# A four-layer encoder in split float32: the output product of each FFN takes both parts of an input tile in one 512-column matmul

## The chip, the cores and the metric

One Trainium2 chip; the kernel runs on one of its NeuronCores. The metric is the device time in microseconds of one execution, and the times given are medians of several timed executions. The engines that matter here are TensorE (PE, with its weight loads as PEld), VectorE (DVE), ScalarE (ACT) and the queue of SyncE (SP) that issues the weight transfers.

## What is computed

Four layers over 256 tokens of width 1024, in float32. Each layer is a half-step SwiGLU FFN, a token mixer (attention, spatial gating, differential attention, attention again) and a second half-step FFN, each between two RMS norms:

```python
D_MODEL, SEQ, DEPTH, D_FF = 1024, 256, 4, 2816

def swiglu(h, w_in, w_out):
    gate, up = jnp.split(h @ w_in, 2, axis=-1)
    return (jax.nn.silu(gate) * up) @ w_out

def reference(x, norm_g, ...):
    for i in range(DEPTH):
        g = norm_g[i]
        x = x + 0.5 * rms_norm(swiglu(rms_norm(x, g[0]), ff1_w_in[i], ff1_w_out[i]), g[1])
        h = rms_norm(x, g[2])
        m = (mixer_a, mixer_b, mixer_c)[i % 3](h, ...)
        x = x + rms_norm(m, g[3])
        x = x + 0.5 * rms_norm(swiglu(rms_norm(x, g[4]), ff2_w_in[i], ff2_w_out[i]), g[5])
    return x
```

The change is in the last product of `swiglu`, which runs eight times (two FFNs in each of four layers).

## The kernel before

Activations lie transposed: 128 features on the partitions, the 256 tokens (`S`) in the free dimension, so a vector of 1024 features is 8 tiles (`KD`) and the hidden layer of 2816 features is 22 tiles (`NJ`). Every large product is made of three: each operand is split into a high part, rounded to the type float32r, and a low part, the rest in the same type, and PE adds high by high, high by low and low by high in PSUM. A matmul takes a 128x128 block of weights as its stationary operand and the 256 tokens of an input tile as its moving operand; each is preceded by its own weight load (LDWEIGHTS).

The weights come as a stream (class `Stream`): SP transfers 1 MB tiles `w_raw` (L104), ACT casts a piece of 1024 columns into `w_hi` (L127), DVE subtracts to get `w_lo` (L130). A piece holds 8 blocks of 128x128. There are 8 slots for split pieces (`SLOTS`); `W.done()` after a piece's last matmul lets ACT and DVE split the piece that goes into the slot made free.

An FFN (`ffn`) has two stages. The first (`project_pair`, L501 and L482) makes gate and up in pairs of tiles; `gate` takes their product and splits the hidden tiles into a high part `hh` (L528, ACT) and a low part `hl` (L529, DVE). They lie in four tiles of SBUF, `h0` and `h1` for the high parts and `l0` and `l1` for the low ones; the mixers use the same four tags for other data. The second stage, which I call the output product, loops over 8 output tiles `d`, and for each over 22 input tiles `k`. `mm3` issues three matmuls for each `k`: `w_hi` by `hh` (L166), `w_lo` by `hh` (L167), `w_hi` by `hl` (L168), 256 columns each. So a stage has 8 x 22 x 3 = 528 matmuls, and because a piece has 8 blocks and a tile 22, piece borders fall inside the tiles at changing places.

When a tile is summed, `Branch.tile_done` has ACT square it out of PSUM (L352) and scale it into `yg` (L353), and DVE adds the square to a running sum (L363). Where a later stage's input can be begun ahead (`Ahead`), ACT and DVE then split two tiles more (L386, L387). After the eighth tile a chain of small steps forms the norm, and the next stage begins with those prepared matmuls (L425 or L427). PSUM tiles of two banks come from a pool of three (`pair()`).

The order of the work on PE, DVE and ACT is the order in which the program is written (`manual_schedule`); each engine runs its own queue in that order and waits on semaphores. `mm3` also serves the last four tiles of the mixers' output product (`project_out`) and one product of `mixer_b`. The gMLP and attention stages have matmuls of other shapes, among them 512-column ones in class `Wide` (L622; an input tile is stationary there and a block of weights of 512 columns moves), and transposes (L694).

Of the kernel before, what the change touches and what calls it, by code (L numbers as in the profile page):

```python
# [16 lines left out]
P = 128  # L17
# [39 lines left out]
def encoder_trunk_kernel(  # L57
# [107 lines left out]
    def mm3(o, ah, al, bh, bl, start, stop, skip=False):  # L165
        nc.tensor.matmul(o, ah, bh, start=start, stop=False, skip_group_check=skip)  # L166
        nc.tensor.matmul(o, al, bh, start=False, stop=False, skip_group_check=skip)  # L167
        nc.tensor.matmul(o, ah, bl, start=False, stop=stop, skip_group_check=skip)  # L168
# [79 lines left out]
    class Normed:  # L248


        def __init__(self, update, gain):
            self.h = act.tile([P, KD, S], F32R, tag="xh", name="xh")
            self.l = act.tile([P, KD, S], F32R, tag="xl", name="xl")
# [86 lines left out]
    class Branch:  # L340


        def __init__(self, gain, n=None, ahead=None):

            self.gain, self.n, self.ahead = gain, n, ahead

        def tile_done(self, d, ps):
            if d == 0:
                self.yg = act.tile([P, KD, S], F32, tag="yg", name="yg")
                self.acc = tmp.tile([P, S], F32, tag="ysq", name="ysq", bufs=1)  # L350
            sq = tmp.tile([P, S], F32, tag="sq1", name="sq1") if d > 0 else self.acc
# [115 lines left out]

    def blocks(piece):
        return [part.rearrange("p (k c) -> p k c", k=KD) for part in piece]

    def project_pair(n, together, between=lambda piece: None, finish=lambda ps: None, most=2, warm=None):

        if together:
            ps = n.ahead.ps
            ws = [blocks(W.peek(i)) for i in range(4)]
            for k, low in JOIN:
                for i in range(4):
# [3 lines left out]
                    for part in ws[i][:1] if low else ws[i]:  # L481
                        nc.tensor.matmul(  # L482
                            o, part[:, k, :], (n.l if low else n.h)[:, k, :],
# [5 lines left out]
        else:  # L489
            ps = pair()  # L490
            for i in range(4):
                wh, wl = blocks(W.peek())
                o = ps[:, i // 2, i % 2 * S:(i % 2 + 1) * S]
                passes = ((wh, n.h), (wh, n.l), (wl, n.h))
# [4 lines left out]
                for at, (k, m) in enumerate(order):  # L499
                    part, xs = passes[m]  # L500
                    nc.tensor.matmul(o, part[:, k, :], xs[:, k, :], start=(at == 0), stop=(at == 3 * KD - 1))  # L501
                    if warm and i == 0:
                        warm(DUMMY[at])
# [7 lines left out]
    def ffn(l, which, update, ahead):  # L511
        n = Normed(update, g_sb[:, l, 4 * which, :])
        hs = [large(tag, (n, S), F32R) for tag, n in (("h0", 16), ("h1", 6), ("l0", 8), ("l1", 14))]

        def hidden(k, n=1):
            h, l = (hs[0], k) if k < 16 else (hs[1], k - 16), (hs[2], k) if k < 8 else (hs[3], k - 8)
            return [t[:, a:a + n, :] for t, a in (h, l)]
# [3 lines left out]
        def gate(jp, ps):  # L521
# [5 lines left out]
            hh, hl = hidden(2 * jp, 2)  # L527
# [24 lines left out]
        for d in range(KD):  # L552
            o = pair()[:, 0, 0:S]
            for k in range(NJ):
                wh, wl = blocks(W.peek())
                hh, hl = hidden(k)
                mm3(o, wh[:, b, :], wl[:, b, :], hh[:, 0, :], hl[:, 0, :], start=(k == 0), stop=(k == NJ - 1))
                b += 1
                if b == KD:
                    if d == KD - 1 and k == NJ - 1:  # L560
# [3 lines left out]
            br.tile_done(d, o)  # L564
# [4 lines left out]
    def project_out(parts, l, between, ahead):  # L569
# [4 lines left out]
        for k, low in ORDER:  # L574
            if not low:
                between(k)
            x = parts(k)[low]
            for (wh, wl), o in zip(ws, os):
                for part in (wh,) if low else (wh, wl):
                    nc.tensor.matmul(  # L580
                        o, part[:, k, :], x, start=(k == 0 and part is wh and not low), stop=(k == KD - 1 and low),
                        skip_group_check=True,
# [7 lines left out]
        for d in range(4, KD):  # L590
            o = pair()[:, 0, 0:S]
            wh, wl = blocks(W.peek())
            for k in range(KD):
                oh, ol = parts(k)
                mm3(o, wh[:, k, :], wl[:, k, :], oh, ol, start=(k == 0), stop=(k == KD - 1))
# [8 lines left out]
    def joined(early, outs):  # L604

        def parts(k, n=None):
            return [x[:, k % 4] if n is None else x[:, k % 4:k % 4 + n] for x in (early if k < 4 else outs)]
# [153 lines left out]
    def mixer_a(l, i, update):  # L761
# [65 lines left out]
        def mix(j):  # L827

            if j == 0:
                t = large("l0", (KD, S), F32R)  # L830
                early.extend((t[:, 0:4], t[:, 4:8]))
# [3 lines left out]
        def between(k):  # L835

            ahead.x_parts(k)
            if k == 0:
                outs.extend(
                    act.tile([P, 4, S], F32R, tag=tag, name=name) for tag, name in (("xh", "oh"), ("xl", "ol"))  # L840
                )
# [13 lines left out]
    def mixer_b(l, i, update):  # L855
# [42 lines left out]
        oh, ol = large("h0", (KD, S), F32R), large("h1", (KD, S), F32R)  # L898
# [29 lines left out]
        for jp in range(KD // 2):  # L928
            ps = pair()
            for e in range(2):  # L930
                wh, wl = blocks(W.peek())
                for k in range(KD):
# [267 lines left out]
```

## Time and profile before

| | |
|---|---|
| median of 3 timed executions | 1996.17 us (1995.66 to 1996.88) |
| the profiled execution's own time | 1993.93 us |
| its span, first to last instruction | 1992.1 us |
| PE busy | 1978.3 us, 16227 matmuls |
| DVE busy | 1279.4 us, 1689 instructions |
| ACT busy | 1081.5 us, 1610 instructions |
| mean granted TensorE clock | 0.998 |
| read from HBM | 347.44 MB, 175 GB/s over the span |

The profile is of one execution, and durations are compared with its own time, not with the median of the others. Matmuls are pipelined: the duration given for one (283 ns for 256 columns) is longer than the distance from its start to the start of the next. What a stream of matmuls costs is therefore read from the distance of starts, and the busy time of PE is the union of overlapping spans. A "granted clock" of 1.0 means 2.4 GHz.

### The profile page before, as it was taken

The page shows a single profiled execution, that of the slowest core. Times are in us where ns is not written, and L with a number is a line of the kernel's source. Part 1 is how long each engine was busy: PE and PEld are TensorE (multiplying, and loading weights), DVE is VectorE, ACT ScalarE, POOL GpSimd, SP SyncE. Part 2 cuts the span into 40 slices and gives each one's busy share as a digit, 9 for nine tenths or more (in the row PEclk, how much of TensorE's full clock was granted, in tenths as well). Part 3 has the DMA queues.
Part 4 walks back from the last instruction along what each step waited for, and adds up shares of the span by engine and source line. Part 5 has one row for each costly group of instructions (what it writes and reads, how often), then busy time and mean ns, then how long its engine had stood idle before and what let it go on. Part 6 is the DMA issues. An engine that isn't in the chain of part 4 may idle for free.

```text
span 1992.1 us, 37700 instructions
## 1 busy us (share of the span) xinstructions
PE 1978.3 (99%) x16227; PEld 1949.1 (98%) x16227; DVE 1279.4 (64%) x1689; ACT 1081.5 (54%) x1610; POOL 6.5 (0%) x21
## 2 busy tenths in 40 slices
PE   9999999999999999999999999999999999999998
PEld 9999999999999989999999999999999999999998
DVE  7655867655765577765665568775566655868553
ACT  6454656545544555645554555764555455666452
POOL 0000000000000000000000000000000000000000
PEclk9999999999999999999999999999999999999999
DMA  7545524645445553645455444254445454525541
GB/s 277 196 170 197 186 99 178 224 169 181 172 177 191 190 173 127 233 170 192 148 194 202 176 151 170 107 225 178 173 154 203 182 192 159 201 113 193 195 184 43
DMA packets 50502, 350.91 MB, mean 176 GB/s; under 512 B 5760, under 2 KB 6016, under 8 KB 9120
## 3 DMA queue, kind: packets, MB, share of 16 engines
q1 hardware_dynamic: 48096, 341.86, 46.7%
q10 hardware_dynamic: 2160, 6.52, 0.9%
q8 instruction: 127, 2.08, 0.4%
q14 instruction: 39, 0.32, 0.0%
q0 software_dynamic: 80, 0.13, 0.0%
HBM read 347.44 MB, written 1.05 MB: 175 GB/s over the span
## 4 chain that ended last, share of the span: by engine, by line
PE 97%; DVE 1%; DMA 1%; ACT 1%; issue 0%; ACTq 0%; SPq 0%; DVEq 0%
PE pp_t L501 54%; PE pp_t L166 9%; PE pp_t L168 9%; PE pp_t L167 9%; PE pp_t L482 3%; PE pp_t L622 3%; PE pp_t L580 2%; PE pp_t L662 1%; DMA w_raw<-in_w 1%; PE pp_t L427 1%; PE pst_t L694 1%; PE pst_t L427 1%; PE pst_t L225 1%; PE pst_t L240 1%; PE pp_t L425 0%; PE pp_t L816 0%
## 5 line engine op out<-in xcount | busy, mean ns | idle before, releaser
L127 ACT CAST w_hi<-w_raw 128x1024 fp32r<-128x1024 f32 (+1 forms) x649 | 670.4, 1047 | 504.5 <-PE pp_t L501 299.3
L130 DVE TENSOR_TENSOR w_lo<-w_raw,w_hi 128x1024 fp32r<-128x1024 f32 (+1 forms) x649 | 774.9, 1219 | 210.1 <-ACT w_hi L127 203.4
L501 PE MATMUL pp_t<-xh,w_hi 128*128 128x256 f32 x2976 | 527.7, 284 | 0.7 <-ACT w_hi L127 0.7
L501 PE MATMUL pp_t<-xl,w_hi 128*128 128x256 f32 x2976 | 524.4, 283 | 0.2 <-DVE xl L316 0.2
L501 PE MATMUL pp_t<-xh,w_lo 128*128 128x256 f32 x2976 | 523.9, 283 | 0.0
L501 PEld LDWEIGHTS pp_t<-xh,w_hi 128*128 128x128 f32 x2976 | 430.1, 192 | 2.6 <-ACT w_hi L127 1.4
L501 PEld LDWEIGHTS pp_t<-xl,w_hi 128*128 128x128 f32 x2976 | 430.7, 192 | 0.7 <-DVE xl L316 0.4
L501 PEld LDWEIGHTS pp_t<-xh,w_lo 128*128 128x128 f32 x2976 | 430.7, 192 | 0.1
L166 PE MATMUL pp_t<-h,w_hi 128*128 128x256 f32 x1456 | 412.0, 283 | 0.0
L167 PE MATMUL pp_t<-h,w_lo 128*128 128x256 f32 x1456 | 412.0, 283 | 0.0
L168 PE MATMUL pp_t<-l,w_hi 128*128 128x256 f32 x1440 | 407.5, 283 | 0.0
L166 PEld LDWEIGHTS pp_t<-h,w_hi 128*128 128x128 f32 x1456 | 279.6, 192 | 0.0
L167 PEld LDWEIGHTS pp_t<-h,w_lo 128*128 128x128 f32 x1456 | 279.6, 192 | 0.0
L168 PEld LDWEIGHTS pp_t<-l,w_hi 128*128 128x128 f32 x1440 | 276.5, 192 | 0.0
L523 DVE TENSOR_TENSOR gs<-pp_t,rbc 128x512 f32<-128x512 f32 x88 | 60.7, 690 | 97.3 <-PE pp_t L501 97.3
L363 DVE TENSOR_TENSOR ysq<-ysq,sq 128x256 f32<-128x256 f32 x72 | 30.6, 425 | 128.4 <-ACT sq L352 128.3
L526 DVE TENSOR_TENSOR hf<-pp_t,gs 128x512 f32<-128x512 f32 x88 | 60.9, 692 | 65.5 <-ACT gs L524 65.5
L529 DVE TENSOR_TENSOR l<-hf,h 128x512 fp32r<-128x512 f32 x88 | 61.0, 693 | 60.4 <-ACT h L528 60.4
L524 ACT ACTIVATE gs<-gs 128x512 f32<-128x512 f32 x88 | 55.6, 632 | 75.7 <-DVE gs L523 75.7
L528 ACT CAST h<-hf 128x512 fp32r<-128x512 f32 x88 | 54.5, 619 | 66.7 <-DVE hf L526 66.7
L301 ACT ACTIVATE xh<-xr,g_sb 128x256 fp32r<-128x256 f32 x96 | 44.8, 504 | 59.4 <-DVE xr L458 56.5
L679 ACT ACTIVATE ex<-s,nm 128x128 f32<-128x128 f32 x96 | 42.7, 448 | 43.1 <-DVE nm L671 24.9
(191 smaller groups left out, 1709.9 us busy)
## 6 DMA issues: line engine op xcount, KB each, us to landing
w_raw<-in_w SPq DMA_DIRECT2D x322, 1024.0 KB, 4.8
l<-in_a_bias ACTq DMA_DIRECT2D x8, 512.0 KB, 7.5
w_raw<-in_w SPq DMA_DIRECT2D x3, 512.0 KB, 7.5
out_y<-xr SPq DMA_DIRECT2D x4, 256.0 KB, 2.5
xr<-in_x_t SPq DMA_DIRECT2D x2, 384.0 KB, 5.8
w_raw<-in_w SPq DMA_DIRECT2D x2, 256.0 KB, 4.3
l<-in_b_ws ACTq DMA_DIRECT2D x1, 512.0 KB, 5.4
l<-in_b_ln_g ACTq DMA_DIRECT2D x1, 512.0 KB, 7.0
```

Source lines behind the costliest of these rows:

```text
L127: nc.scalar.copy(hi[:, cols], raw[:, cols])
L130: nc.vector.tensor_tensor(lo[:, cols], raw[:, cols], hi[:, cols].bitcast(F32), op=ALU.subtract)
L166: nc.tensor.matmul(o, ah, bh, start=start, stop=False, skip_group_check=skip)
L167: nc.tensor.matmul(o, al, bh, start=False, stop=False, skip_group_check=skip)
L168: nc.tensor.matmul(o, ah, bl, start=False, stop=stop, skip_group_check=skip)
L482: nc.tensor.matmul(o, part[:, k, :], (n.l if low else n.h)[:, k, :], start=((k, low) == JOIN[0] and i == 2 and part is ws[i][0]), stop=((k ...
L501: nc.tensor.matmul(o, part[:, k, :], xs[:, k, :], start=(at == 0), stop=(at == 3 * KD - 1))
L523: nc.vector.tensor_tensor(gs, ps[:, :, 0:S], n.bc.unsqueeze(1).broadcast_to([P, 2, S]), op=ALU.mult)
L524: nc.scalar.activation(gs, gs, AF.Silu)
L526: nc.vector.tensor_tensor(hf, ps[:, :, S:2 * S], gs, op=ALU.mult)
L529: nc.vector.tensor_tensor(hl, hf, hh.bitcast(F32), op=ALU.subtract)
L622: nc.tensor.matmul(self.ps[:, t, :], xs[:, kk, t * P:(t + 1) * P], ws, start=((kk, low) == self.order[0] and ws is wh and not (t == 0 and ...
```

## The change

In the output product of the FFN, for its first seven tiles `d`, one matmul with 512 moving columns takes the high and the low part of an input tile together against the same block of `w_hi`; the columns of the high part are summed in one half of a PSUM bank and those of the low part in the other half (`product2`). The matmuls with `w_lo` add to the first half. Within a piece of weights, all 512-column matmuls come first, then all those with `w_lo`. The two halves are added when the tile is done (`Branch.joined`): ACT copies the second half to SBUF, DVE adds it to the first into `yg`, and square and scale then read `yg` in place of PSUM. The eighth tile keeps three matmuls of 256 columns for each input tile (`product`, in the order high by high, high by low, low by high), and no halves to be added.

So that both parts can move in one instruction, they lie side by side: the normed input is one tile `xp` in place of `xh` and `xl`, and the hidden tiles lie as pairs in the four tags by ranges of `k` (0 to 7 in `h0`, 8 to 11 in `h1`, 12 to 15 in `l0`, 16 to 21 in `l1`). The mixers' inputs to their output products are laid out the same way, and where `mm3` served them, `product` does.

```diff
@@ -162,10 +162,24 @@
 
     W = Stream()
 
-    def mm3(o, ah, al, bh, bl, start, stop, skip=False):
-        nc.tensor.matmul(o, ah, bh, start=start, stop=False, skip_group_check=skip)
-        nc.tensor.matmul(o, al, bh, start=False, stop=False, skip_group_check=skip)
-        nc.tensor.matmul(o, ah, bl, start=False, stop=stop, skip_group_check=skip)
+    def product(o, wh, wl, x, ks, at, start, stop):
+
+        for i, k in enumerate(ks):
+            for m, (w_, low) in enumerate(((wh, 0), (wh, 1), (wl, 0))):
+                nc.tensor.matmul(
+                    o, w_[:, at + i, :], x(k)[:, low, :], start=(start and i == 0 and m == 0),
+                    stop=(stop and k == ks[-1] and m == 2),
+                )
+
+    def product2(o, wh, wl, x, ks, at, start, stop):
+
+        for i, k in enumerate(ks):
+            nc.tensor.matmul(o, wh[:, at + i, :], x(k), start=(start and i == 0), stop=False, skip_group_check=True)
+        for i, k in enumerate(ks):
+            nc.tensor.matmul(
+                o[:, 0:S], wl[:, at + i, :], x(k)[:, 0, :], start=False, stop=(stop and k == ks[-1]),
+                skip_group_check=True,
+            )
 
     def pair():
         return pp.tile([P, 2, 512], F32, tag="pp", name="pp_t")
...
@@ -249,8 +263,8 @@
 
 
         def __init__(self, update, gain):
-            self.h = act.tile([P, KD, S], F32R, tag="xh", name="xh")
-            self.l = act.tile([P, KD, S], F32R, tag="xl", name="xl")
+            self.x = act.tile([P, KD, 2, S], F32R, tag="xp", name="xp")
+            self.h, self.l = self.x[:, :, 0, :], self.x[:, :, 1, :]
             acc = tmp.tile([P, 2, S], F32, tag="sqacc", name="sqacc", bufs=1)
             self.acc, self.squares = acc, 0
             self.ahead = update and update.ahead
...
@@ -342,12 +356,22 @@
 
         def __init__(self, gain, n=None, ahead=None):
 
-            self.gain, self.n, self.ahead = gain, n, ahead
+            self.gain, self.n, self.ahead, self.yg = gain, n, ahead, None
+
+        def joined(self, d, o):
+
+            if d == 0:
+                self.yg = act.tile([P, KD, S], F32, tag="yg", name="yg")
+            share = tmp.tile([P, 2, S], F32, tag="upd", name="share")[:, 0, :]
+            nc.scalar.copy(share, o[:, S:2 * S])
+            nc.vector.tensor_tensor(self.yg[:, d, :], o[:, 0:S], share, op=ALU.add)
+            self.tile_done(d, self.yg[:, d, :])
 
         def tile_done(self, d, ps):
             if d == 0:
-                self.yg = act.tile([P, KD, S], F32, tag="yg", name="yg")
                 self.acc = tmp.tile([P, S], F32, tag="ysq", name="ysq", bufs=1)
+                if not self.yg:
+                    self.yg = act.tile([P, KD, S], F32, tag="yg", name="yg")
             sq = tmp.tile([P, S], F32, tag="sq1", name="sq1") if d > 0 else self.acc
             nc.scalar.activation(sq, ps, AF.Square)
             nc.scalar.activation(self.yg[:, d, :], ps, AF.Copy, scale=self.gain[:, d:d + 1])
...
@@ -465,6 +489,10 @@
         n = math.prod(shape)
         return t[:, 0:n].rearrange("p (a b) -> p a b", a=shape[0]) if len(shape) > 1 else t[:, 0:n]
 
+    def pairs(tag, n):
+
+        return act.tile([P, LARGE[tag]], F32R, tag=tag, name=tag)[:, 0:2 * n * S].rearrange("p (k m s) -> p k m s", k=n, m=2)
+
     def blocks(piece):
         return [part.rearrange("p (k c) -> p k c", k=KD) for part in piece]
 
...
@@ -510,11 +538,11 @@
 
     def ffn(l, which, update, ahead):
         n = Normed(update, g_sb[:, l, 4 * which, :])
-        hs = [large(tag, (n, S), F32R) for tag, n in (("h0", 16), ("h1", 6), ("l0", 8), ("l1", 14))]
+        hs = [(a, pairs(tag, n)) for tag, a, n in (("l1", 16, 6), ("l0", 12, 4), ("h1", 8, 4), ("h0", 0, 8))]
 
         def hidden(k, n=1):
-            h, l = (hs[0], k) if k < 16 else (hs[1], k - 16), (hs[2], k) if k < 8 else (hs[3], k - 8)
-            return [t[:, a:a + n, :] for t, a in (h, l)]
+            a, t = next((a, t) for a, t in hs if k >= a)
+            return t[:, k - a:k - a + n]
 
         first = l == 0 and which == 0
 
...
@@ -524,7 +552,8 @@
             nc.scalar.activation(gs, gs, AF.Silu)
             hf = tmp.tile([P, 2, S], F32, tag="hf", name="hf", bufs=3)
             nc.vector.tensor_tensor(hf, ps[:, :, S:2 * S], gs, op=ALU.mult)
-            hh, hl = hidden(2 * jp, 2)
+            h = hidden(2 * jp, 2)
+            hh, hl = h[:, :, 0, :], h[:, :, 1, :]
             nc.scalar.copy(hh, hf)
             nc.vector.tensor_tensor(hl, hf, hh.bitcast(F32), op=ALU.subtract)
 
...
@@ -550,18 +579,27 @@
         br = Branch(g_sb[:, l, 4 * which + 1, :], n, ahead)
         b = 0
         for d in range(KD):
-            o = pair()[:, 0, 0:S]
-            for k in range(NJ):
+            apart = d < KD - 1
+            o = pair()[:, 0, :]
+            k = 0
+            while k < NJ:
+
                 wh, wl = blocks(W.peek())
-                hh, hl = hidden(k)
-                mm3(o, wh[:, b, :], wl[:, b, :], hh[:, 0, :], hl[:, 0, :], start=(k == 0), stop=(k == NJ - 1))
-                b += 1
+                ks = range(k, min(k + KD - b, NJ))
+                k += len(ks)
+                (product2 if apart else product)(
+                    o if apart else o[:, 0:S], wh, wl, lambda i: hidden(i)[:, 0], ks, b, ks[0] == 0, k == NJ
+                )
+                b += len(ks)
                 if b == KD:
-                    if d == KD - 1 and k == NJ - 1:
+                    if d == KD - 1 and k == NJ:
                         W.hold()
                     W.done()
                     b = 0
-            br.tile_done(d, o)
+            if apart:
+                br.joined(d, o)
+            else:
+                br.tile_done(d, o[:, 0:S])
             if ahead:
                 ahead.x_parts(d)
         return br.finish()
...
@@ -590,9 +628,7 @@
         for d in range(4, KD):
             o = pair()[:, 0, 0:S]
             wh, wl = blocks(W.peek())
-            for k in range(KD):
-                oh, ol = parts(k)
-                mm3(o, wh[:, k, :], wl[:, k, :], oh, ol, start=(k == 0), stop=(k == KD - 1))
+            product(o, wh, wl, parts, range(KD), 0, True, True)
             if d == KD - 1:
                 W.hold()
                 W.done()
...
@@ -604,7 +640,8 @@
     def joined(early, outs):
 
         def parts(k, n=None):
-            return [x[:, k % 4] if n is None else x[:, k % 4:k % 4 + n] for x in (early if k < 4 else outs)]
+            x = (early if k < 4 else outs)[0]
+            return x[:, k % 4] if n is None else [x[:, k % 4:k % 4 + n, m, :] for m in range(2)]
         return parts
 
     class Wide:
...
```

The other places of the diff are the same two edits: `n.x[:, k, low, :]` for `n.h` and `n.l`, and tiles of pairs for the inputs that the mixers split (`mixer_b` has its pairs in `h0` alone, `mixer_c` its first four in `h1`).

The start of the first FFN's output product on PE, before: `L166` to `L168` are the matmuls of `mm3`, `h_177` is the tile of high parts and `l_179` that of low parts; the three repeat for every input tile.

```order
L501 MATMUL pp_t<-xh,w_lo 128x256 x8
L166 MATMUL pp_t<-h_177,w_hi 128x256
L167 MATMUL pp_t<-h_177,w_lo 128x256
L168 MATMUL pp_t<-l_179,w_hi 128x256
L166 MATMUL pp_t<-h_177,w_hi 128x256
L167 MATMUL pp_t<-h_177,w_lo 128x256
L168 MATMUL pp_t<-l_179,w_hi 128x256
```

The same place in the changed kernel, the whole first tile and the start of the second; `L177` and `L179` are the two loops of `product2`.

```order
L529 MATMUL pp_t<-xp,w_lo 128x256 x8
L177 MATMUL pp_t<-h_179,w_hi 128x512 x8
L179 MATMUL pp_t<-h_179,w_lo 128x256 x8
L177 MATMUL pp_t<-h_178,w_hi 128x512 x4
L177 MATMUL pp_t<-l_177,w_hi 128x512 x4
L179 MATMUL pp_t<-h_178,w_lo 128x256 x4
L179 MATMUL pp_t<-l_177,w_lo 128x256 x4
L177 MATMUL pp_t<-l_176,w_hi 128x512 x6
L179 MATMUL pp_t<-l_176,w_lo 128x256 x6
L177 MATMUL pp_t<-h_179,w_hi 128x512 x2
L179 MATMUL pp_t<-h_179,w_lo 128x256 x2
```

Sixty-six matmuls of one shape became 22 of 512 columns and 22 of 256, in runs of 8, 8 and 6 that alternate; in the next six tiles the runs are 2, 8, 8, 4; 4, 8, 8, 2; 6, 8, 8; 8, 8, 6; 2, 8, 8, 4; 4, 8, 8, 2.

ACT between the fourth and the sixth tile of the same stage, before: casts of weights, square, scaled copy.

```order
L353 ACTIVATE yg<-pp_t,g_sb 128x256
L386 ACTIVATE ahead<-yg,g_sb 128x256
L127 CAST w_hi<-w_raw 128x1024 x2
L352 ACTIVATE sq_2021<-pp_t 128x256
L353 ACTIVATE yg<-pp_t,g_sb 128x256
L127 CAST w_hi<-w_raw 128x1024 x3
L352 ACTIVATE sq_2106<-pp_t 128x256
```

And in the changed kernel, where `L366` is the copy in `joined`; the square behind it reads what DVE adds in between.

```order
L377 ACTIVATE yg<-yg,g_sb 128x256
L410 ACTIVATE ahead<-yg,g_sb 128x256
L127 CAST w_hi<-w_raw 128x1024 x2
L366 COPY share<-pp_t 128x256
L376 ACTIVATE sq_1925<-yg 128x256
L377 ACTIVATE yg<-yg,g_sb 128x256
L127 CAST w_hi<-w_raw 128x1024 x3
L366 COPY share<-pp_t 128x256
```

One instruction was put ahead of each square, at the same place between the casts.

## Rows read from the trace of the kernel before

**Rows 1.** The page: busy time by engine, and the chain that ended last.

```profile
PE 1978.3 (99%) x16227; PEld 1949.1 (98%) x16227; DVE 1279.4 (64%) x1689; ACT 1081.5 (54%) x1610; POOL 6.5 (0%) x21
...
PE 97%; DVE 1%; DMA 1%; ACT 1%; issue 0%; ACTq 0%; SPq 0%; DVEq 0%
```

**Rows 2.** Instructions of L166 in the first output product: duration min/median/max, first and last start.

```profile
L166 PE MATMUL pp_t<-h,w_hi x176: 283/283/283, 136.1 to 199.1; 128*128 128x256 f32 x176
```

**Rows 3.** The chain of waits in order of time: start us, us, engine, line, count.

```profile
335.04 109.44 PE pp_t L501 x912
...
1176.93 8.84 PE pp_t L622 x39
```

**Rows 4.** The timeline of PE: 512-column matmuls behind 512-column ones, settled.

```profile
204.92 0.62 PE L622 MATMUL pp_t<-w_hi,xh 128*128 128x512 f32 x2
...
206.73 0.61 PE L622 MATMUL pp_t<-w_hi,xl 128*128 128x512 f32 x2
```

**Rows 5.** The timeline of PE where 512-column matmuls follow 256-column ones.

```profile
267.53 1.12 PE L501 MATMUL pp_t<-xh,w_lo 128*128 128x256 f32 x8
268.49 0.63 PE L622 MATMUL pp_t<-w_hi,xh 128*128 128x512 f32 x2
268.96 0.62 PE L622 MATMUL pp_t<-w_lo,xh 128*128 128x512 f32 x2
269.42 0.62 PE L622 MATMUL pp_t<-w_hi,xh 128*128 128x512 f32 x2
...
270.33 0.61 PE L622 MATMUL pp_t<-w_hi,xl 128*128 128x512 f32 x2
...
1239.05 0.63 PE L622 MATMUL pp_t<-w_hi,xh 128*128 128x512 f32 x2
...
1240.89 0.62 PE L622 MATMUL pp_t<-w_hi,xl 128*128 128x512 f32 x2
```

**Rows 6.** The timeline of PE where 256-column matmuls follow 512-column ones.

```profile
213.76 0.28 PE L501 MATMUL pp_t<-xh,w_hi 128*128 128x256 f32 x1
213.87 0.28 PE L501 MATMUL pp_t<-xl,w_hi 128*128 128x256 f32 x1
213.99 0.28 PE L501 MATMUL pp_t<-xh,w_lo 128*128 128x256 f32 x1
...
214.59 0.28 PE L501 MATMUL pp_t<-xl,w_hi 128*128 128x256 f32 x1
```

**Rows 7.** The timeline of PE where 512-column matmuls follow transposes (L694).

```profile
279.51 0.70 PE L622 MATMUL pp_t<-w_hi,xh 128*128 128x512 f32 x2
280.05 0.63 PE L622 MATMUL pp_t<-w_lo,xh 128*128 128x512 f32 x2
...
281.44 0.62 PE L622 MATMUL pp_t<-w_lo,xh 128*128 128x512 f32 x2
```

**Rows 8.** Two output products: us, busy of PE, PEld, DVE, ACT, POOL; clock, DMA share, GB/s.

```profile
136.00:199.40 63.40, 63.40 (x530) 63.40 (x530) 33.67 (x38) 32.35 (x45) 0.00 (x0) 1.00 0.50 179
444.20:507.60 63.40, 63.40 (x531) 63.40 (x530) 35.26 (x42) 34.16 (x49) 0.00 (x0) 1.00 0.50 179
```

**Rows 9.** Waits in the first output product, 136 to 199.4 us: total, times, longest.

```profile
ACT w_hi L127 <- PE pp_t L168: 25.0, 17, 1.8
```

**Rows 10.** Groups by line and form: busy us, mean ns, idle before.

```profile
L437 ACT COPY fy<-pst_t 128x256 f32<-128x256 f32 x7 | 2.5, 353 | 0.0
...
L452 DVE TENSOR_TENSOR upd<-yg,pst_t 128x256 f32<-128x256 f32 x22 | 9.2, 418 | 11.4 <-PE pst_t L240 11.4
...
L130 DVE TENSOR_TENSOR w_lo<-w_raw,w_hi 128x1024 fp32r<-128x1024 f32 x647 | 773.6, 1221 | 209.9 <-ACT w_hi L127 203.4
```

**Rows 11.** The timeline of DVE: the last low part of the hidden tiles.

```profile
139.09 0.69 DVE L529 TENSOR_TENSOR l<-hf,h 128x512 fp32r<-128x512 f32 x1 [0.69 <-ACT h L528]
```

More of the change, by code (lines that the diff above doesn't have):

```diff
@@ L482, in project_pair @@
                         nc.tensor.matmul(
-                            o, part[:, k, :], (n.l if low else n.h)[:, k, :],
+                            o, part[:, k, :], n.x[:, k, int(low), :],
                             start=((k, low) == JOIN[0] and i == 2 and part is ws[i][0]), stop=((k, low) == JOIN[-1]),
@@ L493, in project_pair @@
                 o = ps[:, i // 2, i % 2 * S:(i % 2 + 1) * S]
-                passes = ((wh, n.h), (wh, n.l), (wl, n.h))
+                passes = ((wh, 0), (wh, 1), (wl, 0))
                 if i == 0:
@@ L499, in project_pair @@
                 for at, (k, m) in enumerate(order):
-                    part, xs = passes[m]
-                    nc.tensor.matmul(o, part[:, k, :], xs[:, k, :], start=(at == 0), stop=(at == 3 * KD - 1))
+                    part, low = passes[m]
+                    nc.tensor.matmul(o, part[:, k, :], n.x[:, k, low, :], start=(at == 0), stop=(at == 3 * KD - 1))
                     if warm and i == 0:
@@ L576, in project_out @@
                 between(k)
-            x = parts(k)[low]
+            x = parts(k)
             for (wh, wl), o in zip(ws, os):
@@ L580, in project_out @@
                     nc.tensor.matmul(
-                        o, part[:, k, :], x, start=(k == 0 and part is wh and not low), stop=(k == KD - 1 and low),
-                        skip_group_check=True,
+                        o, part[:, k, :], x[:, int(low), :], start=(k == 0 and part is wh and not low),
+                        stop=(k == KD - 1 and low), skip_group_check=True,
                     )
@@ L829, in mix @@
             if j == 0:
-                t = large("l0", (KD, S), F32R)
-                early.extend((t[:, 0:4], t[:, 4:8]))
+                early.append(pairs("l0", 4))
             if j in (0, 2):
@@ L838, in between @@
             if k == 0:
-                outs.extend(
-                    act.tile([P, 4, S], F32R, tag=tag, name=name) for tag, name in (("xh", "oh"), ("xl", "ol"))
-                )
+                outs.append(act.tile([P, KD, 2, S], F32R, tag="xp", name="op")[:, 0:4])
             if k == 1:
@@ L897, in mixer_b @@
         y = mb[:, 0:2, :].rearrange("p a (g t) -> p (a g) t", t=S)
-        oh, ol = large("h0", (KD, S), F32R), large("h1", (KD, S), F32R)
+        op = pairs("h0", KD)
+        oh, ol = op[:, :, 0, :], op[:, :, 1, :]
         def split(jp):
@@ L931, in mixer_b @@
                 wh, wl = blocks(W.peek())
-                for k in range(KD):
-                    mm3(ps[:, e, 0:S], wh[:, k, :], wl[:, k, :], n.h[:, k, :], n.l[:, k, :], start=(k == 0), stop=(k == KD - 1))
+                product(ps[:, e, 0:S], wh, wl, lambda k: n.x[:, k], range(KD), 0, True, True)
                 if e == 1:
@@ L956, in between @@
                 nc.scalar.preload_act_table(AF.Sqrt)
-        return project_out(lambda k: (oh[:, k, :], ol[:, k, :]), l, between, ahead)
+        return project_out(lambda k: op[:, k], l, between, ahead)
     def mixer_c(l, i, update):
@@ L963, in mixer_c @@
         pt = large("h0", (HC, 3 * P))
-        early, outs = large("h1", (KD, S), F32R), []
-        early = [early[:, 0:4], early[:, 4:8]]
+        early, outs = [pairs("h1", 4)], []
         v = large("l0", (2, D))
@@ L1088, in between @@
             if k == 0:
-                outs.extend(
-                    act.tile([P, 4, S], F32R, tag=tag, name=name) for tag, name in (("xh", "oh"), ("xl", "ol"))
-                )
+                outs.append(act.tile([P, KD, 2, S], F32R, tag="xp", name="op")[:, 0:4])
             if k == 1:
```

## The prediction, before the changed kernel was run

> **What bounds the kernel now.** I read the page first. PE is busy for 99% of the span and carries 97% of the chain that ended last [rows 1]: what counts is how many matmuls PE issues and how far apart they start. Then I looked at the stage that the change rewrites. In the first output product the 176 matmuls of L166 start from 136.1 to 199.1 us [rows 2], which is 63.0 / 175 = 0.360 us for three matmuls, 0.120 us each; the stage is 528 x 0.120 = 63.36 us, and PE is busy for every bit of the 63.40 us around it, with the clock at 1.00 [rows 8]. The other engines are far from the bound there: DVE 33.67 to 35.26 us, ACT 32.35 to 34.16 us [rows 8], and ACT spends 25.0 us of the stage in waiting for PE to free a weight slot [rows 9], so the ring of split weights is full and no one waits for weights.
>
> The chain of waits gives the pace of long undisturbed streams: 912 matmuls of 256 columns in 109.44 us, 0.1200 us each, and 39 of 512 columns in 8.84 us, 0.2267 us each [rows 3]. That is the whole idea of the change: 512 columns cost 0.2267 where twice 256 cost 0.2400. Both fit columns at 2.4 GHz (0.1067 and 0.2133 us) and some 0.0133 us on top, which seems to be paid by the instruction and not by the column.
>
> **The matmuls.** For an input tile the sum falls from 3 x 0.1200 = 0.3600 to 0.2267 + 0.1200 = 0.3467 us, by 0.0133. There are 22 input tiles, 7 of 8 output tiles and 8 FFNs, 1232 in all: 1232 x 0.0133 = **16.4 us less** (2.05 us a stage). All of it lies on the path, since nothing but PE does.
>
> **The alternation.** New are the borders: in a stage, 25 runs of 512 columns behind 256 ones and 25 of the reverse (seventeen runs of 6 or 8, four of 4, four of 2). The trace has both borders, in other stages, and they aren't free. Where 512 columns follow settled 256-column matmuls, the first two start 0.47 us from the pair behind them, the first four take 0.93 and the first eight 1.84 us [rows 5], where eight settled ones take 1.81 [rows 4]. Against n x 0.2267 that is 0.017 for a run of 2, 0.023 for 4, 0.027 for 6 or 8. The second place in the trace gives 1239.05 to 1240.89 us, 1.84 again [rows 5]. So a stage pays 17 x 0.027 + 4 x 0.023 + 4 x 0.017 = 0.62 us, eight stages **5.0 us**. At the reverse border the first two 256-column matmuls take 0.23 us and seven take 0.83, not 0.84 [rows 6]: 0.01 less for each of 200 borders, **2.0 us back** (rows are rounded to 0.01, so 1 to 3). From below the border costs -0.01 us, from above what follows a disturbed start: behind transposes the first eight take 279.51 to 281.44, 1.93 us, 0.117 too many [rows 7]. I take the middle value because its rows have exactly the two shapes of the change, both in settled streams; the outer one has transposes in front. The ends stay for the range.
>
> The Trainium skill has two rules on this distance ("TensorE: Matmul & The Clock Gate", section "Back-to-back issue gap"). One says that an isolated warm matmul costs its columns at 2.4 GHz and 2.5 ns; by it 512 columns would be 215.8 ns, and the saving 1232 x 2.5 ns, an estimate of 3.1 us. The other says that a stream of weight loads and matmuls runs at some 131 ns for 512 columns; by it the saving would be an estimate of 1232 x (240 - 131) ns, 134 us. The trace agrees with neither: it has 0.2267 us, for this type, 39 in a row [rows 3].
>
> **The halves.** For 56 tiles ACT gets one copy of 128x256 out of PSUM, nearest row 0.353 us, and DVE one add of PSUM and SBUF, nearest row 0.418 us [rows 10]. That is 2.5 us of ACT and 2.9 us of DVE in a stage of some 62 us in which they have 26 us and more to spare [rows 8]. New is a wait: ACT's square now waits for DVE's add, which may stand behind one `w_lo` of 1.221 us [rows 10]. Queued behind that square on ACT are the scaled copy, the `ahead` splits and the next casts of weights; the casts come up to 0.353 + 1.221 + 0.418, about 2.0 us, later. A slot made free is needed seven pieces on, 7 x 8 x 0.347 = 19 us later, so nobody waits for it. After the seventh tile the delay is covered by the eighth, 66 x 0.120 = 7.9 us, and the eighth itself is done as before: at the end of the stage, where a chain of small steps does lie on the path, nothing is added. I cost the halves at nothing; were the cover of the eighth tile gone, eight stage ends would pay 2.0 us each, 16 us. A PSUM tile is wanted again three tiles on, over 20 us later.
>
> **The rest.** Hidden tile 20, from the last pair, is first read at 16 x 0.347 + 4 x 0.227 = 6.5 us into the stage, not at 20 x 0.360 = 7.2; its low part is there at 139.78, 3.7 us in [rows 11], so that stays free. The changed order in `product`, the joint tile `xp`, the new ranges of `k` and the mixers' pairs alter addresses and which matmul of a trio comes second, not how many there are: nothing. SP issues the same transfers in the same order; they must come 2 to 3% faster in these stages, where the DMA engines are half idle [rows 8]. PE, ACT and DVE are the only queues in which anything moved.
>
> **The sum.** 16.4 - 5.0 + 2.0 = 13.4 us less. The profiled execution took 1993.93 us, the changed one should take 1980.5, with a span near 1978.7. The median of the timed runs is 2.2 us above that profiled execution, with 1.2 us between highest and lowest; I take the loss of 13.4 from the median: **1982.8 us**.
>
> **Rivals.**
> - *Settled from the start.* The 512-column matmuls run at 0.2267 at once: gain 16.4, or 18.4 with the quick 256-column starts, so 1979.8 to 1977.8 us. For it: behind other 512-column matmuls there is no slow start [rows 4]. Against: both places shown with this border have it, alike to 0.01 us [rows 5].
> - *Never settled.* The runs are only 8 long or less; each may start from a worse state than after a long stream, and the 512s may stay at the 0.2325 of the first four [rows 5]. Loss 1232 x 0.0058 = 7.1, gain 16.4 - 7.1 + 2.0 = 11.3: 1984.9 us; without the quick starts, 1986.9.
> - *Disturbed at each border, so slower.* If the change of shape, together with the wait on a weight piece that comes at the same place, acts like the transposes do, a run of 2 costs 279.51 to 280.05, 0.54 us, 0.087 too many, and longer ones 0.117 [rows 7]: 8 x (21 x 0.117 + 4 x 0.087) = 22.4 us against 16.4. The time is then 2002.2 us. It decides from 16.4 / 200 = 0.082 us a border. Against: waits on pieces occur in the 256-column stage too, every 8 blocks, and cost nothing there [rows 2].
> - *The instruction's share is small.* If only about 2.5 ns of the 13.3 go with the instruction and the rest with the columns or the adding of a second half, the two shapes cost nearly alike and the gain is 1232 x 2.5 ns = 3.1 us: 1993.1 us. The 0.2267 speaks against it [rows 3]. It is the first of the two rules above; the second's 134 us get no chance worth a number.
>
> **How the numbers follow.** Forecast 0.55, settled 0.25, never settled 0.11, disturbed 0.05, small share 0.04. The range goes from the quick end of the settled case, 1977.8, less half a microsecond of scatter, to the poor end of the never-settled one with the same: 1977.3 to 1987.4; it leaves out some 0.1 to 0.15. A change of 0.2%, about 4 us, is what a measurement of this kernel can tell from none. Faster by more than that: the first three cases, 0.91. Within: the small share, 0.04. Slower: the disturbed case, 0.05.
>
> **What would show it.** An output product should take 63.36 - 13.4 / 8, so 61.7 us from its first matmul to its last (61.3 if settled, 62.0 to 62.2 if never), with 1232 matmuls fewer in all, 14995. In it, 512-column matmuls should start 0.233 apart at the head of a run and 0.227 behind it, and the first 256-column ones of a run 0.115. ACT should still wait for PE before its casts. The distance from the stage's last matmul to the next stage's first should be as before. I am wrong if PE shows idle time inside the stage (then the weights or the halves are late), if a border shows distances over 0.3 us (disturbed), or if the gain lies in another stage.

## The result and the profile after

The changed kernel takes **1983.28 us** (median of 4 runs, 1981.81 to 1984.28) against 1996.41 us for the kernel before (median of 4); the ratio is 0.9934 with a 95% interval of 0.9917 to 0.9951. That is 13.1 us less, where 13.4 were forecast, and the gain lies where it was looked for. The profiled execution took 1981.81 us, with a span of 1980.1.

The page of the changed kernel answers to [rows 1]: busy time by engine, and the chain that ended last.

```profile
span 1980.1 us, 35263 instructions
...
PE 1965.4 (99%) x14995; PEld 1884.2 (95%) x14995; DVE 1299.0 (66%) x1745; ACT 1108.3 (56%) x1666; POOL 6.5 (0%) x21
...
PE 97%; DVE 1%; DMA 1%; ACT 0%; issue 0%; ACTq 0%; SPq 0%; DVEq 0%
```

PE is the bound as before, with 1232 matmuls and as many weight loads fewer; the weight loader, which is not the bound, is what got slack. ACT and DVE have 56 instructions more each.

The timeline of PE at the start of the first output product, in the changed kernel (columns: start us, us, engine, line, operation, tiles, shape, count), and the last matmuls of that stage with the first of the small steps behind it:

```profile
136.42 2.00 PE L177 MATMUL pp_t<-h,w_hi 128*128 128x512 f32 x8
138.26 1.12 PE L179 MATMUL pp_t<-h,w_lo 128*128 128x256 f32 x8
139.21 1.09 PE L177 MATMUL pp_t<-h,w_hi 128*128 128x512 f32 x4
140.14 1.07 PE L177 MATMUL pp_t<-l,w_hi 128*128 128x512 f32 x4
141.05 0.64 PE L179 MATMUL pp_t<-h,w_lo 128*128 128x256 f32 x4
...
197.96 0.28 PE L169 MATMUL pp_t<-l,w_lo 128*128 128x256 f32 x1
198.09 0.50 PE L239 MATMUL pst_t<-ones,ysq 128*128 128x1 f32 x4
```

Read distances of starts, not durations. Eight 512-column matmuls take 138.26 - 136.42 = 1.84 us, the very figure of [rows 5]; the eight 256-column ones behind them 0.95, not 0.96; the second eight of 512 columns 1.84 again. The stage lasts from 136.42 to 198.09, 61.67 us, against 63.36 from [rows 2], and all eight stages of the profile are 61.67.

The stretch around it, to be set against [rows 8] (busy of PE, PEld, DVE, ACT, POOL; clock, DMA share, GB/s), and the waits from 136.5 to 198.5 us, against [rows 9]:

```profile
136.00:198.50 62.50, 62.50 (x384) 56.01 (x383) 36.13 (x45) 36.25 (x53) 0.00 (x0) 1.00 0.50 187
```

```profile
DVE yg L367 <- ACT share L366: 14.8, 7, 2.9
ACT w_hi L127 <- PE pp_t L177: 9.7, 8, 1.7
ACT share L366 <- PE pp_t L179: 7.4, 6, 2.0
ACT sq L376 <- DVE yg L367: 2.9, 6, 0.5
```

PE has no idle time in the stage. ACT still waits for PE before it casts, if for less time than before, so the ring of weights is still full. The new wait of ACT's square for DVE's add is there, 0.5 us each time in this stage, and at most 0.493 us over all 56 tiles. DVE's running sum waits for that square in turn, but PE does not.

From each trace I then took the ways between the eight stages, a way being the time from one output product's last matmul (its start and 0.12 us) to the next one's first. "Start" is the way to the first stage, "end" that from the last to the end of the span; the way from 3 to 4 holds `mixer_b`.

| us | start | 1 to 2 | 2 to 3 | 3 to 4 | 4 to 5 | 5 to 6 | 6 to 7 | 7 to 8 | end | one stage |
|---|---|---|---|---|---|---|---|---|---|---|
| before | 136.06 | 244.89 | 130.71 | 212.09 | 130.71 | 243.46 | 130.71 | 244.89 | 11.66 | 63.36 |
| changed | 136.42 | 244.89 | 130.71 | 213.55 | 130.71 | 243.47 | 130.71 | 244.89 | 11.39 | 61.67 |

Six of the nine ways agree to 0.01 us. The stages give 8 x 1.69 = 13.5 us and the end 0.3; the start takes back 0.4 and the way through `mixer_b` 1.5. That makes 12.0 us between the two spans. Whether the 1.5 us belong to the change was the first thing to ask.

### The profile page after: what moved, and what is told of

Its sections match the earlier page's. It is cut to its first block, busy times and chain, and to the rows that moved or that the text cites. A ratio compares the mean times of both kernels' runs of the same rounds, so it can differ in the third digit from the quotient of the medians.

```text
span 1980.1 us, 35263 instructions
## 1 busy us (share of the span) xinstructions
PE 1965.4 (99%) x14995; PEld 1884.2 (95%) x14995; DVE 1299.0 (66%) x1745; ACT 1108.3 (56%) x1666; POOL 6.5 (0%) x21
## 4 chain that ended last, share of the span: by engine, by line
PE 97%; DVE 1%; DMA 1%; ACT 0%; issue 0%; ACTq 0%; SPq 0%; DVEq 0%
PE pp_t L529 54%; PE pp_t L177 14%; PE pp_t L179 7%; PE pp_t L169 6%; PE pp_t L510 3%; PE pp_t L659 3%; PE pp_t L618 2%; PE pp_t L699 1%; DMA w_raw<-in_w 1%; PE pp_t L451 1%; PE pst_t L731 1%; PE pst_t L451 1%; PE pst_t L239 1%; PE pst_t L254 1%; PE pp_t L449 0%; PE pp_t L853 0%
## 5 line engine op out<-in xcount | busy, mean ns | idle before, releaser
L529 PE MATMUL pp_t<-xp,w_hi 128*128 128x256 f32 x5952 | 854.4, 284 | 1.6 <-ACT xp L315 1.0
L529 PEld LDWEIGHTS pp_t<-xp,w_hi 128*128 128x128 f32 x5952 | 787.8, 192 | 3.9 <-ACT xp L315 1.2
L529 PE MATMUL pp_t<-xp,w_lo 128*128 128x256 f32 x2976 | 523.9, 283 | 0.0
L529 PEld LDWEIGHTS pp_t<-xp,w_lo 128*128 128x128 f32 x2976 | 430.7, 192 | 0.0
L177 PE MATMUL pp_t<-h,w_hi 128*128 128x512 f32 x672 | 175.7, 393 | 0.0
L177 PE MATMUL pp_t<-l,w_hi 128*128 128x512 f32 x560 | 147.1, 392 | 0.0
L177 PEld LDWEIGHTS pp_t<-h,w_hi 128*128 128x128 f32 x672 | 117.7, 189 | 17.8
L177 PEld LDWEIGHTS pp_t<-l,w_hi 128*128 128x128 f32 x560 | 100.6, 189 | 17.9
L179 PEld LDWEIGHTS pp_t<-h,w_lo 128*128 128x128 f32 x672 | 97.7, 190 | 10.3
L179 PE MATMUL pp_t<-h,w_lo 128*128 128x256 f32 x672 | 100.5, 282 | 0.0
L179 PEld LDWEIGHTS pp_t<-l,w_lo 128*128 128x128 f32 x560 | 79.6, 190 | 6.0
L179 PE MATMUL pp_t<-l,w_lo 128*128 128x256 f32 x560 | 84.8, 282 | 0.0
L510 PE MATMUL pp_t<-xp,w_hi 128*128 128x256 f32 x378 | 69.2, 283 | 0.0
```

Of the source, the lines that this page charges most:

```text
L177: nc.tensor.matmul(o, wh[:, at + i, :], x(k), start=(start and i == 0), stop=False, skip_group_check=True)
L179: nc.tensor.matmul(o[:, 0:S], wl[:, at + i, :], x(k)[:, 0, :], start=False, stop=(stop and k == ks[-1]), skip_group_check=True,)
L510: nc.tensor.matmul(o, part[:, k, :], n.x[:, k, int(low), :], start=((k, low) == JOIN[0] and i == 2 and part is ws[i][0]), stop=((k, low) = ...
L529: nc.tensor.matmul(o, part[:, k, :], n.x[:, k, low, :], start=(at == 0), stop=(at == 3 * KD - 1))
```

## The experiments

**The layout alone.** All eight output tiles as the eighth.

```diff
-            apart = d < KD - 1
+            apart = False
```

> All eight output tiles as the eighth: three 256-column matmuls for each input tile, no halves; the new layout in pairs and the order of the trio stay. If the gain is that of the 512-column matmuls alone, the time is that of before, 1996.4 us give or take 1, and an output product takes 63.36 us. If the layout by itself moves time, the time differs by more than 2 us: 1998 us if the 1.5 us that the profiled changed kernel lost in mixer_b come from the layout, under 1994 us if the layout brings part of the gain.

1996.39 us (11 runs) against 1997.32 for the kernel before beside it (21 runs); ratio 0.9997, 0.9988 to 1.0006. Every stage is 63.36 us, every way between stages as before, except the one through `mixer_b`: 215.82 us. So the layout in pairs and the new order of the trio bring nothing and cost nothing that the times show (by the interval, at most some 1.2 us), while `mixer_b` took 3.7 us more than in the first profile of before. The timed runs of the same kernel before range from 1995.49 to 1999.06, so executions differ by about as much.

**The halves with 256-column matmuls.** Copy, add and order by pieces as in the changed kernel, but two instructions for one.

```diff
-            nc.tensor.matmul(o, wh[:, at + i, :], x(k), start=(start and i == 0), stop=False, ...)
+            for m in range(2):
+                nc.tensor.matmul(o[:, m * S:(m + 1) * S], wh[:, at + i, :], x(k)[:, m, :],
+                                 start=(start and i == 0 and m == 0), stop=False, ...)
```

> As the changed kernel, but each 512-column matmul is made of two of 256 columns, one for each half of the bank; halves, copy, add and the order by pieces stay. If the halves are free and only the number of instructions counts, the time is that of before, 1996.4 us give or take 1, with 63.36 us for an output product. If the halves cost something at the end of a stage or hold up PE, the time is over 1998 us, and the profile shows PE idle or a longer way from a stage's last matmul to the next stage's first.

1996.97 us (11 runs), ratio 0.9999, 0.9990 to 1.0007. The stages are 63.36 us and the ways between them as before (`mixer_b` 214.89). Everything that the change adds on ACT and DVE is there, and it costs nothing that the times show; without the 512-column instruction the gain is gone.

**The kernel before, profiled again.**

> The kernel before once more, for a second profile. The way from the third output product's end to the fourth's start (the stage that holds mixer_b, 212.1 us in the first profile) was 213.6 to 216.1 us in the five profiles with the new layout. If that is the arrival of weights, which differs from execution to execution, this profile of the unchanged kernel has another value than 212.1 too, by 1 us or more, and everything else as it was. If it is the new layout, it is 212.1 again within 0.3 us.

1995.34 us, one run. The way through `mixer_b` is 213.51 us, 1.42 more than in the first profile of the same kernel; the other ways differ by 0.02 at most. The waits in that stretch (690 to 760 us) name it. First profile of before, second profile of before, changed kernel:

```profile
ACT w_hi L127 <- DMA w_raw<-in_w: 7.0, 1, 7.0
```

```profile
ACT w_hi L127 <- DMA w_raw<-in_w: 8.9, 1, 8.9
```

```profile
ACT w_hi L127 <- DMA w_raw<-in_w: 8.3, 1, 8.3
```

One tile of weights arrives late there, by more or less in each execution. SP issues it at the same time after the third stage's end, 22.59 and 22.78 us without the change and 22.67 with it, so the layout doesn't delay its issue. Its transfer then takes 10.8 and 12.8 us without the change and 12.1 to 14.4 in nine profiles with the new layout, where the median transfer of its size takes 4.8 to 4.9: the two ranges overlap.

A transfer of 1 KB that POOL issues, `row<-rs`, is in flight at the same time. Here it is in the first and second profile of before and in that of the changed kernel (the last figure is the time from issue to landing, in us):

```profile
row<-rs POOLq DMA_DIRECT2D x1, 1.0 KB, 7.5
```

```profile
row<-rs POOLq DMA_DIRECT2D x1, 1.0 KB, 8.8
```

```profile
row<-rs POOLq DMA_DIRECT2D x1, 1.0 KB, 8.7
```

In all eleven profiles the late tile lands 4.1 to 5.2 us after this small transfer has landed, about the time of one ordinary transfer. No run leaves the small transfer out, so that it holds the tile up is likely, not shown.

The way itself was 212.09 and 213.51 us without the change and 213.55 to 216.10 with the new layout. That the unchanged kernel has the same wait, issued at the same time, and moves by 1.4 us is enough to strike the 1.5 us as evidence of a cost. A smaller cost of the layout is not excluded: the two ways without it are the shortest of the eleven, and the intervals of the two experiments above end at 1.0006 and 1.0007, which leaves room for up to 1.4 us, though both medians lie below that of the kernel before.

**The changed kernel again.**

> The changed kernel once more, as the measure for the next two and with more runs: 1983.3 us give or take 1; an output product of 61.67 us. The way through mixer_b varies by 1 us or more from its first 213.55 us if weights arrive at different times, and stays if the layout sets it.

1983.45 us (5 runs, 1980.66 to 1983.98), ratio 0.9928, 0.9914 to 0.9941. Stages 61.67; start 137.35 and `mixer_b` 214.53 in this profile, where they were 136.42 and 213.55, everything else alike.

**One border for each input tile.**

```diff
         for i, k in enumerate(ks):
             nc.tensor.matmul(o, wh[:, at + i, :], x(k), ...)
-        for i, k in enumerate(ks):
             nc.tensor.matmul(o[:, 0:S], wl[:, at + i, :], x(k)[:, 0, :], ...)
```

> As the changed kernel, but for each input tile the 512-column matmul is followed at once by the one with the low weights: 154 borders of each kind in a stage in place of 25. If a border costs by how far the run gets (6 ns for a first 512-column matmul, about 4 back for a single 256-column one), 1232 x 2.3 ns = 2.8 us are lost of the 16.4 and the time is about 1982.8 us, like the changed kernel. If every border costs what the borders of the changed kernel cost on average (25 less 7.5 ns, whatever the length), 1232 x 17.5 ns = 21.6 us are lost and the time is about 2001.6 us.

1989.15 us (4 runs), ratio 0.9960, 0.9947 to 0.9974. Neither figure came: it is 5.7 us worse than the changed kernel, beside which it should have stood by the first, and far better than the constant price of the second. (The kernel before took 0.7 us more beside this run than beside the second run of the changed kernel, so the 5.7 is good to about a microsecond.) The timeline of PE in this kernel, at the start of the first output product:

```profile
136.44 0.28 PE L178 MATMUL pp_t<-h,w_lo 128*128 128x256 f32 x1
136.56 0.40 PE L177 MATMUL pp_t<-h,w_hi 128*128 128x512 f32 x1
136.80 0.28 PE L178 MATMUL pp_t<-h,w_lo 128*128 128x256 f32 x1
136.92 0.40 PE L177 MATMUL pp_t<-h,w_hi 128*128 128x512 f32 x1
...
138.92 0.28 PE L178 MATMUL pp_t<-h,w_lo 128*128 128x256 f32 x1
```

From 136.44 to 138.92 are seven pairs, 2.48 us, 0.354 each where settled ones would take 0.3467. The starts of all eight stages give 0.236 on the mean for a 512-column matmul, later than the first one of a longer run (0.233), and 0.117 for the 256-column one behind it: a border that comes right after another is not priced by its own run alone. The stages are 62.33 us, 1.02 over what settled streams would take, which is 6.6 ns for a pair and 8.2 us in all.

**A whole tile at a time.** All 22 matmuls of 512 columns of a tile, then its 22 with the low weights. A tile touches three or four pieces, and the two or three that it uses up are let go together at its end. The edit, cut to its main lines:

```diff
+            if apart:
+                spots = [divmod(b + i, KD) for i in range(NJ)]
...
+                for i, (a, at) in enumerate(spots):
+                    nc.tensor.matmul(o, parts[a][0][:, at, :], hidden(i)[:, 0], ...)
+                for i, (a, at) in enumerate(spots):
+                    nc.tensor.matmul(o[:, 0:S], parts[a][1][:, at, :], hidden(i)[:, 0, 0, :], ...)
+                br.joined(d, o)
+                gone, b = divmod(b + NJ, KD)
+                W.done(gone)
...
```

> As the changed kernel, but all 22 matmuls of 512 columns of an output tile come first, then its 22 with the low weights, so the pieces of a tile are held until its end: 7 borders of each kind in a stage in place of 25. If the borders cost what the profile of the changed kernel shows (25 ns and 7.5 ns back), 8 x 18 x 17.5 ns = 2.5 us are won: about 1980.8 us, an output product of 61.4 us. If holding three or four of eight pieces starves PE, it shows idle time in the stage and the time is above 1985 us.

The stages are 61.45 us, as the price of the borders says, and still the time is 1986.54 us (5 runs), ratio 0.9948, 0.9936 to 0.9961: about 3 us slower than the changed kernel. The loss is not idle time in the stage, as the second forecast had it. Each of the seven ways from a stage's end is longer: six by 0.64 to 0.93 us, beside that through `mixer_b`. ACT and PE in the timeline at the first stage's end, in this kernel:

```profile
194.11 3.88 ACT L127 CAST w_hi<-w_raw 128x1024 fp32r<-128x1024 f32 x4
200.25 1.05 ACT L127 CAST w_hi<-w_raw 128x1024 fp32r<-128x1024 f32 x1 [2.26 <-DMA w_raw<-in_w]
201.20 0.38 ACT L376 ACTIVATE sq<-pp_t 128x256 f32<-128x256 f32 x1
```

```profile
200.78 0.40 PE L449 MATMUL pp_t<-w_lo,ahead 128*128 128x512 f32 x1
201.63 0.61 PE L239 MATMUL pst_t<-ones,sq 128*128 128x1 f32 x4 [0.45 <-ACT sq L376]
```

With slots freed by twos and threes, the casts come in bunches, the transfers of the next weights too, and a cast waits 2.26 us for a late one. The square of the eighth tile stands behind that cast in ACT's queue, and at the end of a stage PE does wait for it, 0.45 us idle.

**The same with the seventh tile in pieces.** To let the bunch pass before the stage ends, only the first six tiles are taken whole. The edit against the kernel above, cut to its main lines:

```diff
-            if apart:
+            whole = d < KD - 2
+            if whole:
                 spots = [divmod(b + i, KD) for i in range(NJ)]
...
+            if apart and not whole:
+                br.joined(d, o)
```

> Whole tiles of 512-column matmuls for the first six output tiles, pieces in turn for the seventh, the eighth as it was. If the whole-tile kernel lost its gain because its casts bunch before the stage's end and ACT is late for the eighth tile's square, the end is again as in the changed kernel (244.89 and 130.71 us from stage to stage), an output product takes about 61.5 us and the time is 1.4 us under the changed kernel's, about 1982. If the bunching costs there too, the ways from stage to stage stay 0.7 to 0.9 us longer and the time is about 1987 us.

**1981.27 us** (4 runs, 1980.53 to 1981.58), ratio 0.9922, 0.9908 to 0.9936: the lowest median of all kernels here, 2.2 us under the changed kernel beside it, two of whose five runs (1980.66 and 1981.00) are as fast. Stages 61.48, ways between stages 244.89 and 130.71. ACT at the stage's end in this kernel:

```profile
191.78 1.05 ACT L127 CAST w_hi<-w_raw 128x1024 fp32r<-128x1024 f32 x1 [2.52 <-DMA w_raw<-in_w]
192.74 0.37 ACT L366 COPY share<-pp_t 128x256 f32<-128x256 f32 x1
...
194.46 1.98 ACT L127 CAST w_hi<-w_raw 128x1024 fp32r<-128x1024 f32 x2
198.30 0.38 ACT L376 ACTIVATE sq<-pp_t 128x256 f32<-128x256 f32 x1 [1.86 <-PE pp_t L169]
```

The late transfer is there as well, 2.52 us, but it holds up the seventh tile's copy and not the eighth's square, which again waits for PE alone. What the traces show of the gain is 8 x 0.19 = 1.5 us in the stages; the rest is within what executions differ by.

The borders, by four kernels whose stages have the same matmuls and differ in their order alone (if every matmul went at the pace of a long stream, a stage would take 63.36 - 154 x 0.0133 = 61.31 us, called settled below):

| borders of each kind in a stage | 7 | 10 | 25 (changed) | 154 |
|---|---|---|---|---|
| one stage, us | 61.45 | 61.48 | 61.67 | 62.33 |
| above settled, us | 0.14 | 0.17 | 0.36 | 1.02 |
| for one pair of borders, ns | 20 | 17 | 14 | 6.6 |

**The eighth tile in halves too.**

```diff
-            apart = d < KD - 1
+            apart = True
```

> The eighth output tile in halves as well. If its add lies on the path, each of eight stage ends grows by the 0.87 us that stands between a tile's copy and its square in the profile of the changed kernel, against 0.24 us won in the stage: 8 x 0.63 = 5.0 us more, about 1988.3 us. If the matmuls prepared for the next stage cover the add, the time is 1.9 us less, about 1981.4 us.

1986.87 us (4 runs), ratio 0.9951, 0.9937 to 0.9964: slower than the changed kernel by 3.4 us, on the side of the path, with a smaller figure than 5.0. The stage is 61.43 us, 0.24 less as worked out; the ways from a stage's end, but for that through `mixer_b`, grow by 0.70 to 0.73, the end of the program by 0.85. At the first stage's end, ACT and PE:

```profile
198.19 0.37 ACT L366 COPY share<-pp_t 128x256 f32<-128x256 f32 x1 [2.70 <-PE pp_t L179]
199.05 0.42 ACT L376 ACTIVATE sq<-yg 128x256 f32<-128x256 f32 x1 [0.49 <-DVE yg L367]
```

```profile
198.67 0.40 PE L449 MATMUL pp_t<-w_lo,ahead 128*128 128x512 f32 x1
199.52 0.61 PE L239 MATMUL pst_t<-ones,sq 128*128 128x1 f32 x4 [0.46 <-ACT sq L376]
```

The square starts 0.86 us behind the copy, and PE runs out of what it was given for that time: 0.46 us idle. The four small and two prepared matmuls in front of that gap cover only a part.

**Narrower matmuls.**

```diff
-            nc.tensor.matmul(o[:, 0:S], wl[:, at + i, :], x(k)[:, 0, :], ...)
+            for h in range(2):
+                nc.tensor.matmul(o[:, h * P:(h + 1) * P], wl[:, at + i, :], x(k)[:, 0, h * P:(h + 1) * P], ...)
```

> As the changed kernel, but each 256-column matmul with the low weights is made of two of 128 columns with their own weight loads, to see whether an instruction goes on costing its columns and 13.3 ns when it gets narrower. If so, two of 128 cost 0.133 us in place of 0.120 and the time is 1983.4 + 1232 x 0.0133 = 1999.8 us. If a narrow matmul waits for its weight load, two cost what the nearest rows of 128 columns show, 0.109 to 0.112 us each, and the time is 1983.4 + 1232 x 0.100 = about 2107 us.

2113.04 us, one run. The timeline of PE in this kernel:

```profile
138.22 1.90 PE L180 MATMUL pp_t<-h,w_lo 128*128 128x128 f32 x16
139.96 1.16 PE L177 MATMUL pp_t<-h,w_hi 128*128 128x512 f32 x4
140.95 1.08 PE L177 MATMUL pp_t<-l,w_hi 128*128 128x512 f32 x4
```

Sixteen of 128 columns take 1.74 us, 0.109 each on the mean (the second starts 0.059 behind the first, the others some 0.112 apart) and not 0.067: columns and 13 ns are not what bounds a narrow matmul with a weight load of its own. At 256 columns (0.120) a matmul is only a little above that floor. The time is some 6 us over the figure for the load: the 512-column matmuls behind the narrow ones start more slowly too, four in 0.99 us where the changed kernel has 0.93. The Trainium skill ("TensorE: Matmul & The Clock Gate", section "LDWEIGHTS (loading the stationary operand)") gives a weight load the number of its columns divided by 1.2, in ns, which is 107 for 128. The trace's 0.109 to 0.112 us lie close above that, though no run shows by itself that the load is what bounds.

## Why the prediction was right

**The matmuls.** The term was 16.4 us from 1232 x 0.0133. The pace of long streams [rows 3] held in another stage with the operands in other roles. The experiment with two 256-column matmuls for one shows that the gain goes with the number of instructions: same columns, same halves, 63.36 us again. An instruction here is a matmul with its weight load; which of the two carries the 13 ns, no run separates. The rival of a small share, 1993.1 us, is out.

**The alternation.** The term was 3.0 us net, 0.37 us a stage; it measured 61.67 - 61.31 = 0.36. Taken apart by the starts in the eight stages, the 512-column runs lost 4.5 us where 5.0 were forecast and the 256-column ones won back 1.7 where 2.0 were; that the net is closer than either is luck, as the two misses are opposed. The row nearest to the new situation, with exactly these two shapes one behind the other [rows 5], gave the price of a stage to about a hundredth of a microsecond, and the settled rival, 61.3 us a stage, is out, as are the never settled one (62.0 to 62.2) and the disturbed one. What I had not understood is why: that a run is priced by how far it gets holds for runs of 2 to 8, but the kernel with 154 borders, for which I worked out the same loss as for the changed one, lost 1.02 us a stage in place of 0.36. It reads as if what makes a 512-column matmul slow outlasted the single 256-column one behind it. What that is stays open; no run here shows it.

**The halves.** Costed at nothing, and nothing that the times show they cost: 1996.97 us with halves and no wide matmuls, and ways behind the stages as before. The cover of the seventh tile, 7.9 us of the eighth, was enough, and the eighth tile does need its exception. The price without a cover, put at 2.0 us for a stage end, was too high: with the eighth tile in halves the way behind a stage grew by 0.7, because DVE was free for the add (ACT waited 0.49 us, not for a `w_lo` of 1.221 as well) and prepared matmuls covered some of it.

**The rest.** The tile `xp`, the new ranges of `k` and the mixers' pairs: 1996.39 us with all of it and nothing else. The earlier read of the last hidden tiles is not in that kernel; in the changed one PE has no idle time in the stage, so it cost nothing either.

**The sum.** 13.4 us forecast, 13.5 in the stages of the profile, 13.1 between the medians. The trace has one thing that the sum had not: the end of the program is 0.27 us shorter, 11.39 for 11.66, and 11.42 in the second profile. DVE's last step ends 7.82 us behind the stage in both kernels; the difference is in the last store of the output, which lands 2.48 us after its issue and not 2.74. Why, no run shows. The 12.0 us between the two profiled spans would have been a worse witness: they contain the 1.5 us more of the way through `mixer_b`, with its late transfer.

## What to carry to other kernels

When PE is the bound and its matmuls have 256 columns, look for two that share a weight block and have inputs that can lie side by side: each one saved is worth the fixed part of a matmul with its weight load, here 13 ns of 120. Price the new order, not only the new shape, from a place in the trace where the two shapes already meet, and group shapes in long runs as far as the buffers allow. Where a step is added behind a tile, keep the last tile of a stage free of it and of what bunches in the same queue: some 0.7 us more at each of eight ends left the kernel about 3 us slower, a quarter of the gain, although its stages were shorter.

## What the runs showed of the hardware

- A settled stream of float32r matmuls, each with its weight load, starts one every 0.2267 us at 512 columns and 0.1200 at 256; runs of 16 at 128 columns take 0.109 each on the mean, where the columns alone would be 0.053 at 2.4 GHz.
- Where the width changes, the pace is not that of either stream at once: a run of 512 columns loses up to 27 ns over its first five, a run of 256 wins back some 7, and strict alternation costs some 6.6 ns a pair over the sum of the two.
- Between executions of one kernel, nearly all stretches repeat to 0.03 us. In both kernels that were profiled twice, the span differs by what two stretches with waits for transfers differ by: the start (136.0 to 138.7 us over eleven profiles, of several kernels) and `mixer_b` (212.1 to 216.1 us).
- In all eleven profiles a 1 MB weight tile issued beside a 1 KB transfer of POOL took 10.8 to 14.4 us and landed 4.1 to 5.2 us after it; the median for such tiles is 4.8 to 4.9 us. The order is shown, the cause is not.
